# RWKV's outputs and its next state from one run of eight 96-column products

## The chip, the cores and the metric

One core of a Trainium2 chip runs the whole program in one launch. The metric is device time in microseconds (us); TensorE is called PE in the profile, its weight loads PEld, VectorE DVE, ScalarE ACT, GpSimd POOL, and SyncE's DMA issuing SP.

## The reference, cut to what matters

Two sequences, of 1024 and of 2048 tokens, each 1024 wide, go through an even layer and an odd one. The even layer has two branches side by side, an S5 state-space mixer and a bidirectional RWKV-7 mixer of 8 heads of 64, each gated. The odd layer is windowed attention. The change lies in the RWKV mixer, whose recurrence runs over every token, once in each direction:

```python
def step(S, inp):
    r_t, w_t, k_t, v_t, kk_t, b_t = inp
    sa = -jnp.einsum('bhvk,bhk->bhv', S, kk_t)
    S = (S * w_t[:, :, None, :] + sa[..., None] * b_t[:, :, None, :]
         + v_t[..., None] * k_t[:, :, None, :])
    return S, jnp.einsum('bhvk,bhk->bhv', S, r_t)

y = (rwkv_scan(R, tm(heads(decay(0))), K, V, KK, BB, False)
     + rwkv_scan(R, tm(heads(decay(1))), K, V, KK, BB, True))
```

## The kernel before, in words

All arithmetic is in f32. The program has four stages: input projections with the S5 branch, then `mixers`, then the even layer's output, then the odd layer with attention. Only `mixers` is changed. It holds two things: the RWKV recurrence (`rwkv`) and the gate products (`gates`: L887 for the gates, L970 for S5's last product, `h` and `w` being 128 columns wide).

The recurrence is cut into chunks of 32 tokens. The 3072 tokens make 96 chunks in each direction, so 192 in all; a block `h` of 128 tokens has four. For each chunk and each of the 8 heads `u` there is a weight matrix `lt[:, c1, u, :]` of 128 rows and 128 columns, and a right-hand side `rt[:, c1, u, :]` of 128 rows and 64 columns. One half of the rows holds the state, the other half the chunk's 32 values of `v` and 32 solved rows. Before the change the columns of `lt` are: 0 to 31 for the system's right-hand side, 32 to 63 for the outputs, 64 to 127 for the next state. `chain` walks the chunks of one direction in order, and for each one issues

- L1311, "U": eight products of 32 columns (four column groups of the array, each with its own quarter of the output partitions) into `pu`; ScalarE copies the result (L1314);
- L1320, "T": eight 32x32 products with the inverted system; ScalarE copies the solved rows into `rt` in four pieces (L1325);
- L1333 and L1334, "S": eight products of 64 columns, alternately in the two column halves; VectorE multiplies the result by the chunk's decay `wc` and writes it into the next chunk's `rt` (L1340, two instructions).

Beside the chain, `outputs` (L1356, "Y") forms the chunk's outputs: eight products of 32 columns from the same `lt` and `rt` into `pY`; ScalarE copies them into `ys` (L1363), and at a block's fourth chunk four transfers store `ys`. Other PE work of the recurrence is L1186/L1187 (`multiplied`, 64x64 quarters of the array), L1196 (transposes) and L1096 (decays).

In f32 each product appears in the trace as two matmul records and two weight loads, so eight products are 16 records.

The order on each engine is fixed when the program is built. `Plan.run` keeps a clock for each engine and, among the tasks whose inputs are ready, takes by rank and planned start; the gates have the lowest rank, 9. The costs in the `yield` lines are what the plan believes: `CC` 390 ns for U, T and Y, `CS` 620 ns for S, 225 ns for a gate product. `PACE` sets the planned distance between a chain's chunks, in hundredths of a us. `NEED` bears on how readily a gate product is put ahead of more urgent work: it is when the planned columns of PE's recent past come to less.

Of the kernel before, what the change touches and what calls it, by code (L numbers as in the profile page):

```python
# [19 lines left out]
P = 128  # L20
# [65 lines left out]
class Plan:  # L86
# [5 lines left out]
    SLACK = 0.25  # L92
    NEED = 3800
    ISSUE = 0.48
    AFTER = {"PE": 0.28, "SP": 0.0, "ACT": 0.1, "DVE": 0.14, "POOL": 0.1, None: 0.0}

    def __init__(self):
        self.clock = dict.fromkeys(self.AFTER, 0.0)
        self.queue = 0.0
        self.recent = deque()  # L100
        self.tasks = []
        self.now = 0.0
# [12 lines left out]
    def run(self):  # L115
        while self.tasks:
            best = {}
            for task in sorted(self.tasks, key=lambda x: x[0]):
                eng, cost, *waits = task[2]
                ts = [w if isinstance(w, float) else w.t for w in waits]  # L120
                if None in ts:
                    continue
                if eng == "SP":
                    n, cost = cost
                start = max(ts + [self.clock[eng] if eng else 0.0])
                if eng == "PE":
                    cost, cols = cost
                    if task[0] == 9 and eng in best and start <= best[eng][0] + 0.02:
                        end = start + best[eng][1]
                        if sum(c for t, c in self.recent if t > end - 3.413) + best[eng][2][2][1][1] < self.NEED:  # L130
                            best[eng] = start, cost, task
                            continue
                if eng not in best or (start < best[eng][0] and start + cost < best[eng][0] + self.SLACK):
                    best[eng] = start, cost, task
# [9 lines left out]
            else:  # L144
                if eng:
                    self.clock[eng] = start + cost
                if eng == "PE":
                    while self.recent and self.recent[0][0] < start - 4:
                        self.recent.popleft()
                    self.recent.append((start + cost, task[2][1][1]))  # L150
# [320 lines left out]
class Kern:  # L471
# [5 lines left out]
    GH = 2  # L477
    PACE, RF = 900, 9
    PACE2, LEFT = 600, 0
# [8 lines left out]
    RK, RT, RG2 = 1, 1, 2  # L488
    CG, CT, CC, CS, RG = 210, 230, 390, 620, 0
    B1, B2, B3, B4, KD = 2, 3, 1, 2, 0  # L490
# [494 lines left out]
    def rwkv_consts(self, cp):  # L985
# [6 lines left out]
        for d in range(2):  # L992
# [3 lines left out]
            for q in range(4):  # L996
                for c, base in ((0, -1), (32, 0)):
                    blk = tri[32 * q:32 * q + 32, c:c + 32]
                    nc.gpsimd.affine_select(out=blk, in_=blk, pattern=[[sg, 32]], compare_op=ALU.is_ge, fill=0.0, base=base, channel_multiplier=-sg)
# [15 lines left out]
        for i in range(self.NLT):  # L1015
            lt = cp.tile([P, 2, 8, P], F32, name=f"lt{i}")
            for c in range(2):
                nc.scalar.copy(lt[0:64, c, 4:8, 64:P], self.ident[0:64, 0:64].unsqueeze(1).broadcast_to([64, 4, 64]))
                nc.vector.tensor_copy(lt[64:P, c, 0:4, 64:P], self.ident[64:P, 64:P].unsqueeze(1).broadcast_to([64, 4, 64]))
            self.lts.append(lt)  # L1020
# [6 lines left out]
    def rwkv(self, plan, st):  # L1027
# [59 lines left out]
        def decays():  # L1087

            for h in every:
# [32 lines left out]
                h["decays"].mark(t)  # L1122
                tw = yield "DVE", 0.11, t1, ring_wc[d]
                h["wc free"] = ring_wc[d].take(4 if h["prev"] else 3)
                wc = ep.tile([P, 4, 4], F32, name=f"wc{d}", bufs=4)
                nc.vector.tensor_copy(wc, f1[:, :, :, 32 - e])
                h["wc"] = wc
                h["wc in"].mark(tw)

        def scaled():  # L1130

            for h in every:
# [20 lines left out]
                for c2 in range(2):  # L1153
                    cs = self.pair(d, c2)
                    slot, end = None, {}
                    for o in range(2):
                        rows = slice(64 * o, 64 * o + 64)
                        for n, at, off in ((2, 0, b), (0, 32, a)):
                            eng = "POOL" if n == 0 or o < self.APOOL else "DVE"
                            end[eng] = yield eng, 0.72 if eng == "POOL" else 0.455, t, *([] if slot else [ring_lt])  # L1160
                            if not slot:
                                slot, lt = ring_lt.take(2)
                                h["lt"][c2] = lt, slot
# [8 lines left out]
        def multiplied():  # L1172

            again = 0.0
            for i, h in enumerate(every):
                for c2 in range(2):
                    for c1 in range(2):
                        for p in range(4):
                            t = yield "PE", (self.CG / 1000, 128), h["keys"][c2], h["left"][c2], *([] if p else [again, *([] if c1 else [ring_g])])
                            if p == 0:  # L1180
                                again = plan.now + (self.GP / 100 if i > self.GI else 0)
                                if c1 == 0:
                                    gfree = ring_g.take()
                                    g = pg.tile([P, 2, 4, 64], F32, name="pg")
                                    (kb, kfree), (lt, _) = h["kb"][c2], h["lt"][c2]
                            nc.tensor.matmul(g[64:P, c1, p], kb[0:64, p, c1].rearrange("c s i -> c (s i)"), lt[0:64, c1, 4 + p, 0:64], start=True, stop=True)  # L1186
                            nc.tensor.matmul(g[0:64, c1, p], kb[64:P, p, c1].rearrange("c s i -> c (s i)"), lt[64:P, c1, p, 0:64], start=True, stop=True)  # L1187
                    plan.add(self.RK, masked(h, c2, g, lt, t, gfree))
# [14 lines left out]
        def masked(h, c2, g, lt, t, gfree):  # L1203
            t = yield "DVE", 1.3, t
            for rows, us in parts:
                nc.vector.tensor_tensor(lt[rows, :, us, 0:64], g[rows], self.tri[h["d"]][rows].unsqueeze(1).unsqueeze(1).broadcast_to([64, 2, 4, 64]), MULT)  # L1206
            gfree.mark(t)
# [3 lines left out]
        def turned(h, c2, g, lt, t, gfree):  # L1211
            for c1 in range(2):
                t = yield "ACT", 0.76, t
                for o, (rows, us) in enumerate(parts):
                    nc.scalar.copy(lt[rows, c1, us, 64:P], g[64 * c1:64 * c1 + 64, :, 64 * o:64 * o + 64])
                h["chunk"][2 * c2 + (c1 if h["d"] == 0 else 1 - c1)].mark(t)
            gfree.mark(t)

        def gathered(h, c2):
# [4 lines left out]
            for q in range(4):  # L1224
# [3 lines left out]
                put(win["ng"][32 * q:32 * q + 32, sys:sys + 4, :].rearrange("s (n j) t -> s n j t", j=2),  # L1228
                    lt[32 * q:32 * q + 32, :, 2 * q:2 * q + 2, 0:32])
            win["full"].mark(t)  # L1230
# [39 lines left out]
        def rights(hs):  # L1270

            for h in hs:
# [3 lines left out]
                for c2 in range(2):  # L1276
                    t = yield "POOL", 0.95, ring_rt[d]
                    rt = rp.tile([P, 2, 8, 64], F32, name=f"rt{d}")
                    h["rt"][c2] = rt, ring_rt[d].take(2)
                    nc.gpsimd.memset(rt, 0.0)  # L1280
# [12 lines left out]
        def chain(hs):  # L1293

            state = again = 0.0
            for h in hs:
# [3 lines left out]
                for ci in range(4):  # L1300
# [7 lines left out]
                    for j in range(2):  # L1308
                        for q in range(4):
                            u = 2 * q + j  # L1310
                            nc.tensor.matmul(pu[32 * q:32 * q + 32, j, :], lt[:, c1, u, 0:32], rt[:, c1, u, :], start=True, stop=True)  # L1311
                    t = yield "ACT", 0.26, t
# [10 lines left out]
                    for q in range(4):  # L1323
                        rows = slice(32 * q, 32 * q + 32)
                        nc.scalar.copy(rt[rows, c1, 2 * q:2 * q + 2, :], pu[rows, 2:4])  # L1325
                    plan.add(1, outputs(h, ci, c4, t, (ltfree, rtfree) if ci % 2 else ()))
                    nh = h if ci < 3 else h["next"]
                    if nh:
                        ni = (ci + 1) % 4
                        n4 = nat(ni)  # L1330
                        t = yield "PE", (self.CS / 1000, 1024), t
                        for p in range(4):
                            nc.tensor.matmul(pu[0:64, 4 + p, :], lt[:, c1, 4 + p, 64:P], rt[:, c1, 4 + p, :], start=True, stop=True)  # L1333
                            nc.tensor.matmul(pu[64:P, 4 + p, :], lt[:, c1, p, 64:P], rt[:, c1, p, :], start=True, stop=True)  # L1334
# [7 lines left out]
                    if ci % 2:  # L1342
                        ltfree.mark(t)
                        rtfree.mark(t)

        def outputs(h, ci, c4, t, frees):
            s, d, ti = h["s"], h["d"], h["ti"]
            c1, c2 = c4 % 2, ci // 2
            lt, rt = h["lt"][c2][0], h["rt"][c2][0]
# [7 lines left out]
            for x in frees:  # L1357
                x.mark(t)
            t = yield "ACT", 0.27, t, *([] if ci else [ring_ys[d]])
            if ci == 0:  # L1360
                h["y"] = ep.tile([P, 4, P], F32, name=f"ys{d}", bufs=1)
# [784 lines left out]
```

## Time and profile before

| what | value |
|---|---|
| median of 3 runs | 4057.42 us (4056.36 to 4058.29) |
| profiled execution: its time | 4065.39 us |
| its span | 4063.7 us |
| PE busy, share of the span | 3763.6 us, 93% |
| mean granted PE clock | 0.97 of full speed |

The profiled execution took 1.7 us more than its span, and 8 us more than the median of the runs. Busy PE time counts overlapping matmuls once.

### The profile page before, as it was taken

The numbers are of one execution on the slowest core, as the hardware profiler recorded it, in microseconds if no ns is written. First come the engines' busy times: TensorE is split into PE (matmuls) and PEld (weight loads), VectorE is DVE, ScalarE is ACT, GpSimd is POOL, SyncE is SP. The second block draws the span as 40 slices with busy tenths as digits, with TensorE's granted clock in tenths as the row PEclk, the third lists the DMA queues.
The fourth block names the chain that finished last, engine by engine and source line by source line (L and its number), as shares of the span: only waits on it lengthen the run. The fifth ranks groups of instructions, "written<-read, shape, count | busy, mean of one in ns | idle before, by whom it ended". The sixth has DMA issues, their size and how long they took to land.

```text
span 4063.7 us, 87721 instructions
## 1 busy us (share of the span) xinstructions
PE 3763.6 (93%) x34128; PEld 3118.4 (77%) x34128; DVE 2821.8 (69%) x5545; ACT 1939.8 (48%) x4847; POOL 1615.8 (40%) x2007
## 2 busy tenths in 40 slices
PE   6878999999899999999998799999999999999999
PEld 4656766676688888878876577999999977778777
DVE  8356655666568878888887676544444469899997
ACT  3334333333345565555655322333323357777776
POOL 4422322232364555555540242222222335555554
PEclk9989999999999999999999899999999999999999
DMA  5677565566543334333344666644444422222221
GB/s 154 162 174 228 162 191 173 174 191 188 176 154 101 119 112 127 119 106 115 119 115 98 216 233 214 206 148 155 143 157 147 147 84 72 77 81 74 76 66 58
DMA packets 536324, 570.32 MB, mean 140 GB/s; under 512 B 93602, under 2 KB 436770, under 8 KB 525924
## 3 DMA queue, kind: packets, MB, share of 16 engines
q1 hardware_dynamic: 535908, 564.72, 45.4%
q8 instruction: 268, 4.39, 0.5%
q14 instruction: 148, 1.21, 0.1%
HBM read 398.03 MB, written 166.56 MB: 139 GB/s over the span
## 4 chain that ended last, share of the span: by engine, by line
PE 45%; DVE 17%; DMA 4%; issue 4%; POOL 3%; ACT 2%; SPq 1%; DVEq 0%; ACTq 0%; POOLq 0%
PE ps L412 30%; DVE sb L412 11%; PE acc L887 5%; PE pc L1333 2%; PE acc L970 2%; PE pg L1186 2%; ACT sb L412 2%; DMA rk<-rk 1%; DVE ng L1251 1%; DVE z L1253 1%; PE pY L1356 1%; PE pc L1320 1%; POOL lt L1165 1%; PE pc L1311 1%; DVE lt L1206 1%
## 5 line engine op out<-in xcount | busy, mean ns | idle before, releaser
L412 PE MATMUL ps<-sb 128*128 128x512 f32 (+8 forms) x12464 | 2542.2, 359 | 153.2 <-DVE sb L412 48.4
L412 PEld LDWEIGHTS ps<-sb 128*128 128x128 f32 (+2 forms) x12464 | 1958.8, 187 | 555.7 <-DVE sb L412 105.0
L412 POOL TENSOR_TENSOR sb<-sb,sb 128x384 f32<-128x384 f32 (+5 forms) x468 | 469.5, 1021 | 444.2 <-ACT sb L412 226.0
L412 POOL TENSOR_TENSOR sb<-sb 128x512 f32<-128x512 f32 (+5 forms) x358 | 320.7, 899 | 675.0 <-ACT sb L412 325.8
L412 DVE TENSOR_TENSOR sb<-ps,sb 128x512 fp32r<-128x512 f32 (+4 forms) x620 | 402.0, 661 | 189.7 <-PE ps L412 115.5
L412 POOL TENSOR_TENSOR sb<-sb,mhalf 128x8 f32<-128x8 f32 (+3 forms) x156 | 223.0, 1431 | 644.4 <-DVE sb L412 640.5
L887 PE MATMUL acc<-h,w 128*128 128x128 f32 x3072 | 448.0, 290 | 17.0 <-POOL rt L1280 14.3
L887 PEld LDWEIGHTS acc<-h,w 128*128 128x128 f32 x3072 | 383.1, 196 | 42.5 <-POOL rt L1280 14.5
L412 ACT ACTIVATE sb<-sb 128x256 fp32r<-128x256 f32 (+9 forms) x392 | 276.1, 710 | 286.3 <-DVE sb L412 128.5
L412 ACT COPY sb<-ps 128x512 f32<-128x512 f32 (+4 forms) x402 | 195.1, 502 | 438.0 <-PE ps L412 429.3
L412 PE MATMUL ps<-ident,sb 128*128 128x128 f32 x1888 | 317.2, 280 | 55.5 <-DVE sb L412 51.1
L412 DVE TENSOR_TENSOR sb<-sb,sb 128x256 fp32r<-128x256 f32 (+6 forms) x259 | 265.8, 1038 | 142.9 <-ACT sb L412 128.8
L412 ACT ACTIVATE sb<-sb,sb 128x384 f32<-128x384 f32 (+3 forms) x486 | 299.3, 619 | 111.5 <-DVE sb L412 60.4
L412 PEld LDWEIGHTS ps<-ident,sb 128*128 128x128 f32 x1888 | 237.6, 143 | 119.9 <-DVE sb L412 72.1
L1165 POOL TENSOR_TENSOR lt<-rk,lb 64x256 f32<-64x256 f32 x288 | 216.9, 761 | 196.3 <-PE pY L1356 84.8
L412 ACT ACTIVATE sb<-ps 128x512 f32<-128x512 f32 x108 | 64.5, 597 | 385.7 <-PE ps L412 385.7
L1325 ACT COPY rt<-pc 32x128 f32<-32x128 f32 x768 | 196.7, 256 | 97.7 <-PE pc L1320 86.6
L412 DVE CUSTOM_DVE_ANT_0 sb<-ps,sb,sb 128x384 f32<-128x384 f32 (+1 forms) x384 | 215.3, 588 | 28.6 <-PE ps L412 27.1
L1150 POOL TENSOR_TENSOR kb<-rk,f 128x128 f32<-128x128 f32 x384 | 197.6, 546 | 76.1 <-PE pg L1196 67.6
L412 ACT CAST sb<-ps 128x512 fp32r<-128x512 f32 x368 | 202.1, 587 | 50.9 <-PE ps L412 46.0
L1340 DVE TENSOR_TENSOR rt<-pc,wc 64x256 f32<-64x256 f32 x376 | 158.3, 421 | 71.5 <-PE pc L1334 36.1
L412 DVE TENSOR_SCALAR sb<-sb,sb 128x384 f32<-128x384 f32 (+4 forms) x264 | 190.6, 751 | 18.2 <-POOL sb L412 16.2
(121 smaller groups left out, 4680.1 us busy)
## 6 DMA issues: line engine op xcount, KB each, us to landing
sb<-wsp SPq DMA_DIRECT2D x65, 1024.0 KB
rk<-rk SPq DMA_DIRECT2D x96, 512.0 KB
sb<-in_od_w_in SPq DMA_DIRECT2D x36, 1024.0 KB
h<-h SPq DMA_DIRECT2D x48, 512.0 KB
sb<-in_od_w_z SPq DMA_DIRECT2D x24, 1024.0 KB
qkv<-sb SPq DMA_DIRECT2D x72, 256.0 KB
sb<-qkv SPq DMA_DIRECT2D x72, 256.0 KB
sb<-in_x_sample SPq DMA_DIRECT2D x32, 512.0 KB
```

The costliest lines, as they stand in the source:

```text
L412: self.ops.append((eng, self.cost(eng, op, outs[-1] if outs[-1] is not k.get("accum_out") else outs[0], ins, a, k), deps, self.rank, lambd ...
L887: nc.tensor.matmul(sums[n][1][:, m * P:m * P + P], w[:, k, m * P:m * P + P], acts[n][0][:, k], start=k == 0, stop=k == KT - 1)
L970: nc.tensor.matmul(ps[:, 256 * (m % 2):256 * (m % 2) + 256], uw_at(k)[:, m], act_at(n)[:, 2 * k:2 * k + 2], start=k == 0, stop=k == 3)
L1150: nc.gpsimd.tensor_tensor(kb[:, sl, :, x, :], arr[n][:, sl, cs], f1[:, sl, cs, a:a + 32], MULT)
L1165: (nc.gpsimd if eng == "POOL" else nc.vector).tensor_tensor(ltv[:, :, :, at:at + 32], arr[n][rows, :, cs], f2[rows, :, cs, off:off + 32], ...
L1186: nc.tensor.matmul(g[64:P, c1, p], kb[0:64, p, c1].rearrange("c s i -> c (s i)"), lt[0:64, c1, 4 + p, 0:64], start=True, stop=True)
L1206: nc.vector.tensor_tensor(lt[rows, :, us, 0:64], g[rows], self.tri[h["d"]][rows].unsqueeze(1).unsqueeze(1).broadcast_to([64, 2, 4, 64]), MULT)
L1251: nc.vector.tensor_tensor(tv, z[:, 0:k, k:k + 1].broadcast_to([P, k, 31 - k]), z[:, k:k + 1, k + 1:32].broadcast_to([P, k, 31 - k]), MULT)
L1253: nc.vector.tensor_tensor(z[:, 0:k, k + 1:32], z[:, 0:k, k + 1:32], tv, ADD)
L1325: nc.scalar.copy(rt[rows, c1, 2 * q:2 * q + 2, :], pu[rows, 2:4])
L1333: nc.tensor.matmul(pu[0:64, 4 + p, :], lt[:, c1, 4 + p, 64:P], rt[:, c1, 4 + p, :], start=True, stop=True)
L1340: nc.vector.tensor_tensor(nrt[rows, n4 % 2, 4 - 4 * o:8 - 4 * o, :], pu[rows, 4:8], nh["wc"][rows, :, n4:n4 + 1].broadcast_to([64, 4, 64]) ...
```

## The change

The columns of `lt` are turned round: the next state's 64 columns now stand first, then 32 for the outputs, then 32 for the right-hand side of the system. S and Y become one run, Z: for each of the 8 heads one product of 96 columns into 96 partitions of a full PSUM bank `pz`, rows 0 to 63 the next state, rows 64 to 95 the outputs. VectorE reads the state for both head groups from partitions 0 to 63, so the decay `wc` is kept on 64 partitions and is filled by two copies. ScalarE copies the outputs as 32 partitions of 512 columns into the block's row of `ys`, which one transfer then stores. In the plan, Z costs `CS` 900 ns and 2048 columns, a PE task costs `TURN` 95 ns more when it is 128-wide work (gates or Z) behind other work or the other way round, `NEED` is 3000, `PACE` 800, and the store is planned 0.5 us behind the copy and no longer 2.0.

```diff
-    NEED = 3800
+    NEED = 3000
+    TURN = 0.095
...
+                    cost += self.TURN * (self.wide != (task[0] == 9 or cols == 2048))
...
+                    self.wide = task[0] == 9 or task[2][1][1] == 2048
...
-    PACE, RF = 900, 9
+    PACE, RF = 800, 9
...
-    CG, CT, CC, CS, RG = 210, 230, 390, 620, 0
+    CG, CT, CC, CS, RG = 210, 230, 390, 900, 0
+    YL = 0.5
...
-                tw = yield "DVE", 0.11, t1, ring_wc[d]
+                tw = yield "DVE", 0.22, t1, ring_wc[d]
...
-                wc = ep.tile([P, 4, 4], F32, name=f"wc{d}", bufs=4)
-                nc.vector.tensor_copy(wc, f1[:, :, :, 32 - e])
+                wc = ep.tile([64, 2, 4, 4], F32, name=f"wc{d}", bufs=4)
+                for o in range(2):
+                    nc.vector.tensor_copy(wc[:, o], f1[64 * o:64 * o + 64, :, :, 32 - e])
...
-                    plan.add(1, outputs(h, ci, c4, t, (ltfree, rtfree) if ci % 2 else ()))
+                    t = yield "PE", (self.CS / 1000, 2048), t, ring_y
+                    yfree = ring_y.take(2)
+
+                    pz = py.tile([P, 8, 64], F32, name="pz")
+                    for u in range(8):
+                        nc.tensor.matmul(pz[0:96, u, :], lt[:, c1, u, 0:96], rt[:, c1, u, :], start=True, stop=True)
+                    if ci % 2:
+                        ltfree.mark(t)
+                        rtfree.mark(t)
+                    plan.add(1, outputs(h, ci, c4, pz, t, yfree))
...
-                        t = yield "PE", (self.CS / 1000, 1024), t
-                        for p in range(4):
-                            nc.tensor.matmul(pu[0:64, 4 + p, :], lt[:, c1, 4 + p, 64:P], rt[:, c1, 4 + p, :], start=True, stop=True)
-                            nc.tensor.matmul(pu[64:P, 4 + p, :], lt[:, c1, p, 64:P], rt[:, c1, p, :], start=True, stop=True)
-                        tm = t
                         state = t = yield "DVE", 0.87, t, nh["wc in"], nh["right"][ni // 2]
                         nrt = nh["rt"][ni // 2][0]
                         for o in range(2):
-                            rows = slice(64 * o, 64 * o + 64)
-                            nc.vector.tensor_tensor(nrt[rows, n4 % 2, 4 - 4 * o:8 - 4 * o, :], pu[rows, 4:8], nh["wc"][rows, :, n4:n4 + 1].broadcast_to([64, 4, 64]), MULT)
+                            us = slice(4 - 4 * o, 8 - 4 * o)
+                            nc.vector.tensor_tensor(nrt[64 * o:64 * o + 64, n4 % 2, us, :], pz[0:64, us], nh["wc"][:, o, :, n4:n4 + 1].broadcast_to([64, 4, 64]), MULT)
                         nh["wc free"].mark(t)
...
-            t = yield "PE", (self.CC / 1000, 512), t, ring_y
-            yfree = ring_y.take()
-            pY = py.tile([P, 2, 64], F32, name="pY")
-            for j in range(2):
-                for q in range(4):
-                    u = 2 * q + j
-                    nc.tensor.matmul(pY[32 * q:32 * q + 32, j, :], lt[:, c1, u, 32:64], rt[:, c1, u, :], start=True, stop=True)
...
-            t = yield "ACT", 0.27, t, *([] if ci else [ring_ys[d]])
+            t = yield "ACT", 0.53, t, *([] if ci else [ring_ys[d]])
...
-            nc.scalar.copy(h["y"][:, c4, :], pY.rearrange("r j v -> r (j v)"))
+            nc.scalar.copy(h["y"][32 * c4:32 * c4 + 32], pz[64:96].rearrange("i u v -> i (u v)"))
...
-                t = yield "SP", (4, 0.73), t + 2.0
-                dst = self.sp[s]["y"][d][ti].rearrange("(n i) c -> i n c", i=32)
-                for q in range(4):
-                    nc.sync.dma_start(dst[:, :, q * P:(q + 1) * P], h["y"][32 * q:32 * q + 32])
+                t = yield "SP", (1, 0.73), t + self.YL
+                nc.sync.dma_start(self.sp[s]["y"][d][ti], h["y"])
```

Left out of this diff are the lines that only follow the new order of the columns (the masks `tri`, the identity blocks in `lt`, the slices in `scaled`, `multiplied`, `masked`, `turned`, `gathered` and U) and the counts of readers of `lt` and `rt`, which fall from two to one.

## Rows read from the trace of the kernel before

**Rows 1.** The profile's page: span, busy time of each engine.
```profile
span 4063.7 us, 87721 instructions
...
PE 3763.6 (93%) x34128; PEld 3118.4 (77%) x34128; DVE 2821.8 (69%) x5545; ACT 1939.8 (48%) x4847; POOL 1615.8 (40%) x2007
```

**Rows 2.** Windows: us; busy PE, PEld, DVE, ACT, POOL; PEclk; DMA share; GB/s.
```profile
1245.00:2268.00 1023.00, 961.71 (x18161) 798.52 (x18162) 833.34 (x1736) 600.04 (x1913) 484.02 (x744) 0.97 0.39 112
...
1250.00:2050.00 800.00, 762.76 (x14873) 648.93 (x14873) 672.15 (x1406) 474.10 (x1538) 439.62 (x685) 0.98 0.38 116
```

**Rows 3.** TensorE's timeline (start, duration, work): one place, first and last state runs.
```profile
1251.70 0.27 PE L1333 MATMUL pc<-rt,lt 128*64 128x64 f32 x1
...
1611.87 0.27 PE L1333 MATMUL pc<-rt,lt 128*64 128x64 f32 x1
...
1611.97 0.22 PE L1333 MATMUL pc<-rt,lt 128*64 128x64 f32 x1
...
1612.32 0.22 PE L1333 MATMUL pc<-rt,lt 128*64 128x64 f32 x1
...
1612.48 0.43 PE L1356 MATMUL pY<-rt,lt 128*32 128x64 f32 x16
1612.84 0.94 PE L887 MATMUL acc<-h,w 128*128 128x128 f32 x6
1613.71 0.43 PE L1311 MATMUL pc<-rt,lt 128*32 128x64 f32 x16
...
2049.30 0.27 PE L1333 MATMUL pc<-rt,lt 128*64 128x64 f32 x1
```

**Rows 4.** The same timeline elsewhere: two kinds alike in line, a longer gate run.
```profile
1608.53 0.43 PE L1311 MATMUL pc<-rt,lt 128*32 128x64 f32 x16
1608.78 0.41 PE L1356 MATMUL pY<-rt,lt 128*32 128x64 f32 x16
1609.11 0.71 PE L887 MATMUL acc<-h,w 128*128 128x128 f32 x4
...
1619.88 2.05 PE L887 MATMUL acc<-h,w 128*128 128x128 f32 x16
1621.86 0.27 PE L1333 MATMUL pc<-rt,lt 128*64 128x64 f32 x1
```

**Rows 5.** TensorE's timeline: 128-column weights under two streamed columns, two places.
```profile
562.62 0.72 PE L412 MATMUL ps<-heads,sb 128*128 128x2 f32 x6
563.21 2.74 PE L412 MATMUL ps<-sb 128*128 128x512 f32 x14
...
1077.00 1.17 PE L412 MATMUL ps<-heads,sb 128*128 128x2 f32 x10
1078.04 2.29 PE L412 MATMUL ps<-sb 128*128 128x512 f32 x9
```

**Rows 6.** Lines L1333 and L887: weight loads, ns least, median, most.
```profile
L1333 PEld LDWEIGHTS pc<-rt,lt x1504: 132/138/232, 1245.7 to 2261.0; 128*64 128x64 f32 x188
...
L887 PEld LDWEIGHTS acc<-h,w x3072: 186/192/338, 1114.1 to 2073.7; 128*128 128x128 f32 x192
```

**Rows 7.** Groups by line and form: busy us, mean ns, idle before.
```profile
L1325 ACT COPY rt<-pc 32x128 f32<-32x128 f32 x768 | 196.7, 256 | 97.7 <-PE pc L1320 86.6 <-DMA twt<-tw 1.1 <-DMA rt<-v 1.0
...
L1340 DVE TENSOR_TENSOR rt<-pc,wc 64x256 f32<-64x256 f32 x376 | 158.3, 421 | 71.5 <-PE pc L1334 36.1 <-issue 15.1 <-ACT rt L1325 9.8
...
L412 ACT COPY sb<-ps 64x512 f32<-64x512 f32 x96 | 55.8, 581 | 31.0 <-PE ps L412 29.1
...
L1363 ACT COPY ys<-pY 128x128 f32<-128x128 f32 x192 | 50.6, 265 | 88.9 <-PE pY L1356 71.1 <-issue 5.9 <-DMA y<-ys 5.7
...
L1126 DVE COPY wc<-f 128x16 f32<-128x16 f32 x48 | 12.8, 266 | 0.8 <-ACT f L1117 0.4
```

**Rows 8.** Waits by engine and line: us in total, times, longest.
```profile
POOL rt L1280 <- PE pY L1356: 104.7, 18, 18.1
```

**Rows 9.** Transfers issued between 1400 and 2000 us.
```profile
y<-ys SPq DMA_DIRECT2D x111, 64.0 KB
```

More of the change, by code (lines that the diff above doesn't have):

```diff
@@ L100, in __init__ @@
         self.recent = deque()
+        self.wide = False
         self.tasks = []
@@ L996, in rwkv_consts @@
             for q in range(4):
-                for c, base in ((0, -1), (32, 0)):
+                for c, base in ((32, -1), (0, 0)):
                     blk = tri[32 * q:32 * q + 32, c:c + 32]
@@ L1017, in rwkv_consts @@
             for c in range(2):
-                nc.scalar.copy(lt[0:64, c, 4:8, 64:P], self.ident[0:64, 0:64].unsqueeze(1).broadcast_to([64, 4, 64]))
-                nc.vector.tensor_copy(lt[64:P, c, 0:4, 64:P], self.ident[64:P, 64:P].unsqueeze(1).broadcast_to([64, 4, 64]))
+                nc.scalar.copy(lt[0:64, c, 4:8, 0:64], self.ident[0:64, 0:64].unsqueeze(1).broadcast_to([64, 4, 64]))
+                nc.vector.tensor_copy(lt[64:P, c, 0:4, 0:64], self.ident[64:P, 64:P].unsqueeze(1).broadcast_to([64, 4, 64]))
             self.lts.append(lt)
@@ L1157, in scaled @@
                         rows = slice(64 * o, 64 * o + 64)
-                        for n, at, off in ((2, 0, b), (0, 32, a)):
+                        for n, at, off in ((2, 96, b), (0, 64, a)):
                             eng = "POOL" if n == 0 or o < self.APOOL else "DVE"
@@ L1161, in scaled @@
                             if not slot:
-                                slot, lt = ring_lt.take(2)
+                                slot, lt = ring_lt.take()
                                 h["lt"][c2] = lt, slot
@@ L1185, in multiplied @@
                                     (kb, kfree), (lt, _) = h["kb"][c2], h["lt"][c2]
-                            nc.tensor.matmul(g[64:P, c1, p], kb[0:64, p, c1].rearrange("c s i -> c (s i)"), lt[0:64, c1, 4 + p, 0:64], start=True, stop=True)
-                            nc.tensor.matmul(g[0:64, c1, p], kb[64:P, p, c1].rearrange("c s i -> c (s i)"), lt[64:P, c1, p, 0:64], start=True, stop=True)
+                            nc.tensor.matmul(g[64:P, c1, p], kb[0:64, p, c1].rearrange("c s i -> c (s i)"), lt[0:64, c1, 4 + p, 64:P], start=True, stop=True)
+                            nc.tensor.matmul(g[0:64, c1, p], kb[64:P, p, c1].rearrange("c s i -> c (s i)"), lt[64:P, c1, p, 64:P], start=True, stop=True)
                     plan.add(self.RK, masked(h, c2, g, lt, t, gfree))
@@ L1205, in masked @@
             for rows, us in parts:
-                nc.vector.tensor_tensor(lt[rows, :, us, 0:64], g[rows], self.tri[h["d"]][rows].unsqueeze(1).unsqueeze(1).broadcast_to([64, 2, 4, 64]), MULT)
+                nc.vector.tensor_tensor(lt[rows, :, us, 64:P], g[rows], self.tri[h["d"]][rows].unsqueeze(1).unsqueeze(1).broadcast_to([64, 2, 4, 64]), MULT)
             gfree.mark(t)
@@ L1214, in turned @@
                 for o, (rows, us) in enumerate(parts):
-                    nc.scalar.copy(lt[rows, c1, us, 64:P], g[64 * c1:64 * c1 + 64, :, 64 * o:64 * o + 64])
+                    nc.scalar.copy(lt[rows, c1, us, 0:64], g[64 * c1:64 * c1 + 64, :, 64 * o:64 * o + 64])
                 h["chunk"][2 * c2 + (c1 if h["d"] == 0 else 1 - c1)].mark(t)
@@ L1228, in gathered @@
                 put(win["ng"][32 * q:32 * q + 32, sys:sys + 4, :].rearrange("s (n j) t -> s n j t", j=2),
-                    lt[32 * q:32 * q + 32, :, 2 * q:2 * q + 2, 0:32])
+                    lt[32 * q:32 * q + 32, :, 2 * q:2 * q + 2, 96:P])
             win["full"].mark(t)
@@ L1278, in rights @@
                     rt = rp.tile([P, 2, 8, 64], F32, name=f"rt{d}")
-                    h["rt"][c2] = rt, ring_rt[d].take(2)
+                    h["rt"][c2] = rt, ring_rt[d].take()
                     nc.gpsimd.memset(rt, 0.0)
@@ L1310, in chain @@
                             u = 2 * q + j
-                            nc.tensor.matmul(pu[32 * q:32 * q + 32, j, :], lt[:, c1, u, 0:32], rt[:, c1, u, :], start=True, stop=True)
+                            nc.tensor.matmul(pu[32 * q:32 * q + 32, j, :], lt[:, c1, u, 96:P], rt[:, c1, u, :], start=True, stop=True)
                     t = yield "ACT", 0.26, t
@@ L1338, in chain, with outputs @@
                         for o in range(2):
-                            rows = slice(64 * o, 64 * o + 64)
-                            nc.vector.tensor_tensor(nrt[rows, n4 % 2, 4 - 4 * o:8 - 4 * o, :], pu[rows, 4:8], nh["wc"][rows, :, n4:n4 + 1].broadcast_to([64, 4, 64]), MULT)
+                            us = slice(4 - 4 * o, 8 - 4 * o)
+                            nc.vector.tensor_tensor(nrt[64 * o:64 * o + 64, n4 % 2, us, :], pz[0:64, us], nh["wc"][:, o, :, n4:n4 + 1].broadcast_to([64, 4, 64]), MULT)
                         nh["wc free"].mark(t)
[L1342 to L1346, printed above, removed]
+                    yfree.mark(t)
+        def outputs(h, ci, c4, pz, t, yfree):
             s, d, ti = h["s"], h["d"], h["ti"]
-            c1, c2 = c4 % 2, ci // 2
-            lt, rt = h["lt"][c2][0], h["rt"][c2][0]
-            t = yield "PE", (self.CC / 1000, 512), t, ring_y
-            yfree = ring_y.take()
-            pY = py.tile([P, 2, 64], F32, name="pY")
-            for j in range(2):
-                for q in range(4):
-                    u = 2 * q + j
-                    nc.tensor.matmul(pY[32 * q:32 * q + 32, j, :], lt[:, c1, u, 32:64], rt[:, c1, u, :], start=True, stop=True)
-            for x in frees:
-                x.mark(t)
-            t = yield "ACT", 0.27, t, *([] if ci else [ring_ys[d]])
+            t = yield "ACT", 0.53, t, *([] if ci else [ring_ys[d]])
             if ci == 0:
-                h["y"] = ep.tile([P, 4, P], F32, name=f"ys{d}", bufs=1)
+                h["y"] = ep.tile([P, 512], F32, name=f"ys{d}", bufs=1)
                 h["y free"] = ring_ys[d].take()
-            nc.scalar.copy(h["y"][:, c4, :], pY.rearrange("r j v -> r (j v)"))
+            nc.scalar.copy(h["y"][32 * c4:32 * c4 + 32], pz[64:96].rearrange("i u v -> i (u v)"))
             yfree.mark(t)
             if ci == 3:
-                t = yield "SP", (4, 0.73), t + 2.0
-                dst = self.sp[s]["y"][d][ti].rearrange("(n i) c -> i n c", i=32)
-                for q in range(4):
-                    nc.sync.dma_start(dst[:, :, q * P:(q + 1) * P], h["y"][32 * q:32 * q + 32])
+                t = yield "SP", (1, 0.73), t + self.YL
+                nc.sync.dma_start(self.sp[s]["y"][d][ti], h["y"])
                 h["y free"].mark(t)
```

## The prediction

> **What bounds the kernel now.** I read the page first, then windows over the stage that changes, then PE's timeline inside it. The page says that PE is busy for 93% of the span and no other engine for more than 69% [rows 1]. The windows say the same of the changed stage: the recurrence runs from 1245 to 2268 us, 1023 us for 96 chunks in each direction, so 10.66 us for one step of both chains, and PE is busy for 961.7 us of it. 61 us are left over. VectorE is busy for 833, ScalarE for 600, POOL for 484 [rows 2]. The granted clock is 0.97 there. So in this stage time follows what PE has to do, and the change must be priced in PE time between the start of one run of products and the start of the next. Busy time won't do for that, as neighbouring records overlap.
>
> The timeline gives those starts. S begins at 1611.87, its second pair comes 0.10 later, and from 1611.97 to the last pair at 1612.32 six steps take 0.35, so 0.058 us for a pair; Y begins at 1612.48, so S takes 0.61. Y to the gate run behind it takes 0.36 [rows 3]. Where U is followed by Y, of the same shape, U takes only 0.25 [rows 4]: 0.11 of the 0.36 is the change to another kind of product. A gate run of six records takes 0.87 up to U [rows 3], one of sixteen 1.98 up to S [rows 4]: 0.111 for a record, and 0.87 - 6 x 0.111 = 0.20 that does not grow with the run, 0.10 for each of its two changes of kind.
>
> **What a chunk costs on PE now.** S 0.61 and Y 0.36, of which 0.11 is saved where U follows. Counted in the timeline from 1250 to 2050 us, of 148 S runs [rows 3] 103 have 128-wide work ahead of them, and of 148 Y runs 74 have it behind them and 19 have U. With 0.10 for each change out of or into 128-wide work: 0.61 + 0.10 x 103/148 + 0.36 - 0.11 x 19/148 + 0.10 x 74/148 = 0.61 + 0.07 + 0.35 + 0.05 = 1.08 us. That is what goes.
>
> **What Z costs.** The run has 16 records, each of 96 weight columns under 64 streamed columns. No such record is in the trace, so it is bounded from both sides. If the stream sets the pace, a record costs what 64 columns cost in S, 0.058, and Z 16 x 0.058 = 0.93. If the weight load sets the pace, the row to ask is one with many weight columns and hardly any stream. There is one: the norm's products with `heads`, 128 weight columns under two streamed ones. Six records take 0.59 us and ten 1.04 [rows 5], so four more take 0.45, 0.112 for a record: as much as a gate record, which streams 128 columns. Two columns cannot take that long to stream; the load of 128 weight columns does, and the next record waits for it. The duration of one load grows from 138 ns for 64 columns to 192 ns for 128 [rows 6], 0.84 ns for a column, so 96 columns should take 32 x 0.84 = 27 ns less than 128: 0.112 - 0.027 = 0.085 for a record and 16 x 0.085 = 1.36 us for Z. Until now the narrow products hid this, since S and Y load two and four column groups beside each other: S has 64 columns in each half and still needs only 0.058 for two records [rows 3].
>
> A rule speaks against the change: the Trainium skill, "TensorE: Matmul & The Clock Gate", section "LDWEIGHTS (loading the stationary operand)", gives a load's time as the number of its columns divided by 1.2 per ns, whatever the number of rows. As an estimate from that page Z would be 16 x 80 ns = 1.28 us in place of my 1.36, and the loss below smaller by 15 us; the rows above are longer by some 5 ns a record than the rule, and the sum goes by them.
>
> I take 1.36, since the `heads` row is the one case here in which the load has no stream to hide behind; 0.93 stays as the lower bound. Upper bound: if 96 columns load no faster than 128, 16 x 0.112 = 1.79. I give that little, as load times do follow the columns [rows 6].
>
> Z is 128-wide like the gates, so changes of kind go where Z stands beside them. With the neighbours of S and Y as counted, 45/148 of the Z runs have narrow work ahead and half have it behind: 0.10 x 0.30 + 0.10 x 0.50 = 0.08. Z with its changes: 1.44. PE gains 1.44 - 1.08 = 0.36 us for a chunk, and 192 chunks make +70 us.
>
> **What of that is time.** Of the 61 us in which PE stands idle in this stage [rows 2], a part goes if PE itself is later than its suppliers: the plan believes in 0.9 us plus 0.095 for a change, so POOL, VectorE and the loads are laid out for a PE that is faster than the real one. Not all goes, as the last chunks wait on their own chain. I take half, 30 us: +70 - 30 = +40. None and all of it are the bounds: +70 and +9.
>
> **The other parts.** ScalarE's copy of the outputs goes from 128x128 at 265 ns to 32 rows of 512; the nearest row is a 64x512 copy at 581 ns [rows 7]. That is 192 x 0.32 = 61 us more on an engine that is idle for 423 of the 1023 us [rows 2]. It costs nothing while it lies beside PE. Queued behind it are the copies of U and T of the other chain: if each such copy held up a chain, a step of 10.66 us would still have room. That step needs U 0.36, its copy 0.27, T 0.36, four copies of 0.256, Z 1.44 and two VectorE products of 0.42 [rows 3, 7], 4.3 us and the handovers. VectorE has 48 more small copies of `wc`, 0.27 each [rows 7], 13 us off the path. SP issues 3 x 48 = 144 transfers fewer; the stores were 64 KB each [rows 9] and are one of 256 KB for a block now. The store is issued 1.5 us earlier in the plan; if the copy is late, SP waits, and behind it stand the loads of `rk`, `v` and the gates' activations. I put the two together at nothing, and at 10 us either way for the range. `lt` and `rt` come free behind Z and not behind the later Y; POOL's clearing of `rt` waited 104.7 us for Y [rows 8], but POOL is busy for under half of the stage, so what it gains is slack. `PACE` 800 asks for 8 us between chunks where PE delivered 10.66: it moves recurrence ahead of gates and takes no work off PE. The two VectorE products read PSUM in the same sizes as before, 0.
>
> **The sum.** The profiled execution took 4065.4 us; with +40 it is 4105. The runs' median lies 8 us below it, so the forecast is 4057.4 + 40 = 4097 us.
>
> **The rivals.** *The stream sets the pace after all (other side).* Then Z is 0.93 + 0.08 = 1.01 against 1.08, -0.07 for a chunk, and between 128-wide neighbours 0.93 against 0.10 + 0.61 + 0.36 + 0.10 = 1.17, -0.24: -13 to -46 us, so 4011 to 4044, middle 4028. For it speaks that changes of kind cost a real 0.10, measured in the gate runs, and that each Z saves one or two of them. Against it stands the `heads` row. It decides from the record's price: with 1.08 - 0.08 = 1.00 us left for 16 records, Z breaks even at 0.0625 us a record before any idle time is absorbed, and at about 0.072 with it (30 us over 192 chunks are 0.16 us).
>
> *The load sets the pace, but it doesn't show.* All 61 us of idle time go, or the plan, retimed, puts gates on both sides of Z: then 1.36 against 1.17, +0.19 x 192 = +36, less what is absorbed. 4052 to 4065.
>
> *Worse: the clock.* `NEED` 3000 puts fewer gate products ahead of the chain, and PE's mix of work changes with Z. If the stage's granted clock fell from 0.97 [rows 2] to 0.93, that is 4% of 1023 us, 41 us on top: 4138.
>
> **How the numbers follow.** A change within 0.2% (8 us) cannot be told from none here. Load-bound Z with half of the idle time taken, 0.54: 4066 to 4127 by the bounds, slower. Stream-bound Z, 0.31: faster. Load hidden by slack, 0.10: the same in 0.08, slower in 0.01, faster in 0.01. Clock, 0.05: slower. Faster 0.32, same 0.08, slower 0.60. The range from 4025 to 4128 takes in the likeliest case and more than half of the rival below it, and leaves out the lower end of that rival and the clock. The likeliest case's own range is 4066 to 4127.
>
> **What would show each step.** Z's records: 0.085 us apart, or 0.058. Z from start to next start beside the gates 1.36. No gap between Z and a gate run. PE busy in the stage above 94% and the stage from 1245 us on longer by some 40 us, with the other stages as they are. ScalarE's copy at about 0.58. The chain's step above 10.66 us with its waits still on PE. I am wrong if Z takes under 1.0 us, or if the stage's time doesn't follow PE's work.

## The result and the profile after

The changed kernel takes 4144.47 us (median of 4 runs, 4141.55 to 4150.86) against 4056.89 for the kernel before, run beside it: a ratio of 1.0216, 95% interval 1.0201 to 1.0231. That is 87.6 us slower, where 40 were forecast, and beyond the range. The profiled execution took 4143.15 us, 77.8 more than that of before.

The page, a window over the stretch of [rows 2], and the groups by line and form:

```profile
span 4141.2 us, 81618 instructions
...
PE 3815.2 (92%) x31120; PEld 3223.2 (78%) x31120; DVE 2850.2 (69%) x5593; ACT 2002.3 (48%) x4847; POOL 1589.1 (38%) x2007
```
```profile
1245.00:2268.00 1023.00, 950.00 (x14656) 850.32 (x14655) 815.72 (x1702) 622.21 (x1824) 460.91 (x743) 0.97 0.34 104
```
```profile
L1361 ACT COPY ys<-pz 32x512 f32<-32x512 f32 x192 | 110.7, 578 | 186.4 <-DVE rt L1351 87.1 <-PE pz L1338 83.4 <-PE pc L1318 5.9
...
L1133 DVE COPY wc<-f 64x16 f32<-64x16 f32 x96 | 27.4, 285 | 1.9 <-ACT f L1123 1.1
```

Two things stand against each other. PE has more work: 51.6 us more busy time in the whole program [rows 1]. Yet in the changed stage it is *less* busy than before, 950 us of the 1023 against 961.7 [rows 2]. The granted clock is 0.97 as before. So PE got more to do and was kept from doing it; the forecast had only the first.

TensorE's timeline shows one Z run from its start to the next start, and the lines of Z's load, of S5's last product (L976; L970 before) and of U show where the stage ends:

```profile
1606.92 1.49 PE L1338 MATMUL pz<-rt,lt 128*96 128x64 f32 x16
1608.34 0.27 PE L1193 MATMUL pg<-lt,kb 64*64 64x64 f32 x1
```
```profile
L1338 PEld LDWEIGHTS pz<-rt,lt x3072: 159/165/283, 1235.8 to 2282.1; 128*96 128x96 f32 x192
...
L976 PE MATMUL acc<-w x384: 379/379/796, 2203.0 to 2347.6; 128*128 128x256 f32 x192
...
L1318 PE MATMUL pc<-rt,lt x3072: 216/219/316, 1137.4 to 2278.3; 128*32 128x64 f32 x192
```

Z takes 1.42 here (ahead of narrow work it is either 1.42 or 1.50), and 1.33 as the median of some 60 runs that stand between 128-wide work: 0.083 us for a record. Its load lies between those of [rows 6]. The recurrence's last U starts at 2278.3. In the kernel before, the same two lines read:

```profile
L970 PE MATMUL acc<-w x384: 379/379/796, 2077.4 to 2256.3; 128*128 128x256 f32 x192
...
L1311 PE MATMUL pc<-rt,lt x3072: 216/219/316, 1143.4 to 2265.1; 128*32 128x64 f32 x192
```

There the last U starts at 2265.1, and S5's product was done before the recurrence ended, its last record at 2256.3; now that record starts at 2347.6. So the two chains end only 13 us later, but the low-ranked products that fill their gaps no longer fit in them, and the last of them run behind the chains for some 70 us.

The waits hold something that [rows 7] doesn't have. ScalarE's copy of the outputs waits for VectorE, and VectorE for ScalarE's copy:

```profile
ACT ys L1361 <- DVE rt L1351: 87.1, 61, 4.6
...
DVE rt L1351 <- ACT ys L1361: 51.3, 57, 4.2
...
PEld pc L1327 <- ACT u L1321: 36.9, 45, 3.9
...
PE pc L1327 <- ACT u L1321: 27.2, 35, 3.7
```

Both engines read the same PSUM bank `pz`, VectorE rows 0 to 63 and ScalarE rows 64 to 95, and the program lets one go only when the other is through. In the kernel before they read two tiles, `pu` and `pY`. PE comes into it in the last two rows: T waits for ScalarE's copy of U, 27.2 us in all. In the kernel before that wait was small:

```profile
PE pc L1320 <- ACT u L1314: 3.6, 7, 0.9
```

A stretch of the timeline of all engines shows how:

```profile
1549.57 1.49 PE L1338 MATMUL pz<-rt,lt 128*96 128x64 f32 x16
...
1550.49 0.71 DVE L1260 TENSOR_TENSOR z<-z,ng 128x220 f32<-128x220 f32 x1
1550.99 0.43 PE L1318 MATMUL pc<-rt,lt 128*32 128x64 f32 x16
1551.13 0.41 DVE L878 SCALAR_TENSOR_TENSOR z<-z,acc 128x256 f32<-128x256 f32 x1
1551.46 0.62 DVE L1258 TENSOR_TENSOR ng<-z 128x228 f32<-128x228 f32 x1
...
1551.57 0.38 ACT L876 ACTIVATE z<-acc 128x256 f32<-128x256 f32 x1 [1.76 <-DVE z L878]
...
1552.33 0.84 DVE L1351 TENSOR_TENSOR rt<-pz,wc 64x256 f32<-64x256 f32 x2
...
1553.26 0.58 ACT L1361 COPY ys<-pz 32x512 f32<-32x512 f32 x1 [1.31 <-DVE rt L1351]
...
1553.86 0.27 ACT L1321 COPY u<-pc 128x128 f32<-128x128 f32 x1
...
1554.18 0.53 PE L1327 MATMUL pc<-u,tt 32*32 32x64 f32 x16 [2.15 <-ACT u L1321]
```

Z ends at about 1551.0. VectorE still has other work in its queue and reads the state only from 1552.33 to 1553.17. ScalarE ends a gate's activation at 1551.95 and could copy the outputs then, but stands for 1.31 us until VectorE is through; behind that copy in its queue stands the copy of U, whose product has been done since 1551.4, and behind that T on PE, which idles for 2.15 us.

### The profile page after: what moved, and what is told of

The parts are those of the page before. It is cut to its first block, busy times and chain, and to the rows that moved or that the text cites. A ratio compares the mean times of both kernels' runs of the same rounds, so it can differ in the third digit from the quotient of the medians.

```text
span 4141.2 us, 81618 instructions
## 1 busy us (share of the span) xinstructions
PE 3815.2 (92%) x31120; PEld 3223.2 (78%) x31120; DVE 2850.2 (69%) x5593; ACT 2002.3 (48%) x4847; POOL 1589.1 (38%) x2007
## 5 line engine op out<-in xcount | busy, mean ns | idle before, releaser
L893 PE MATMUL acc<-h,w 128*128 128x128 f32 x3072 | 429.7, 287 | 16.3 <-DMA w<-in_ev_w_zr 14.0
L1338 PE MATMUL pz<-rt,lt 128*96 128x64 f32 x3072 | 299.7, 252 | 0.2 <-ACT rt L1332 0.2
L1338 PEld LDWEIGHTS pz<-rt,lt 128*96 128x96 f32 x3072 | 287.4, 169 | 6.8 <-ACT rt L1332 0.4
L1351 DVE TENSOR_TENSOR rt<-pz,wc 64x256 f32<-64x256 f32 x376 | 156.2, 415 | 134.0 <-PE pz L1338 75.8
L417 DVE CUSTOM_DVE_ANT_0 sb<-ps,sb,sb 128x384 f32<-128x384 f32 (+1 forms) x384 | 215.5, 588 | 27.2 <-PE ps L417 25.5
L1157 POOL TENSOR_TENSOR kb<-rk,f 128x128 f32<-128x128 f32 x384 | 178.8, 496 | 133.3 <-PE pg L1203 106.5
```

The lines of the kernel that those rows point to most:

```text
L417: self.ops.append((eng, self.cost(eng, op, outs[-1] if outs[-1] is not k.get("accum_out") else outs[0], ins, a, k), deps, self.rank, lambd ...
L893: nc.tensor.matmul(sums[n][1][:, m * P:m * P + P], w[:, k, m * P:m * P + P], acts[n][0][:, k], start=k == 0, stop=k == KT - 1)
L1157: nc.gpsimd.tensor_tensor(kb[:, sl, :, x, :], arr[n][:, sl, cs], f1[:, sl, cs, a:a + 32], MULT)
L1338: nc.tensor.matmul(pz[0:96, u, :], lt[:, c1, u, 0:96], rt[:, c1, u, :], start=True, stop=True)
L1351: nc.vector.tensor_tensor(nrt[64 * o:64 * o + 64, n4 % 2, us, :], pz[0:64, us], nh["wc"][:, o, :, n4:n4 + 1].broadcast_to([64, 4, 64]), MULT)
```

## The experiments

The theories: *(L)* the weight load makes Z long, and PE's time is the program's; *(P)* the plan's numbers (`CS`, `NEED`, `PACE`, `TURN`) made a worse order; *(B)* the bank that two engines read costs waits that the plan does not hold. The runs were made on other chips, where the kernel before took 4070 to 4075 us, so only ratios to the kernel before on the same chip are compared; 0.01 is 41 us.

**Z without the long load (z32).** Three products of 32 columns in three column groups, in place of one of 96, all else as after:
```diff
-                        nc.tensor.matmul(pz[0:96, u, :], lt[:, c1, u, 0:96], rt[:, c1, u, :], start=True, stop=True)
+                        for e in range(0, 96, 32):
+                            nc.tensor.matmul(pz[e:e + 32, u, :], lt[:, c1, u, e:e + 32], rt[:, c1, u, :], start=True, stop=True)
```


> Only Z's products change: each 96-column product becomes three of 32 columns, in three column groups beside each other; plan, order, buffers and all other work stay. If the weight loads set Z's price (0.083 us a record, 1.33 us a run), three short loads run side by side and the run costs what its stream costs, 16 x 0.058 = 0.93 plus about 0.13 for leaving the kind, and more changes against the gates: some 0.25 to 0.3 us less a chunk, 45 to 60 us in all, about 4090 us. If instead the stream or the bank of eight heads set it, Z stays near 1.4 us and the time near 4144.

Ratio 1.0175 (1.016 to 1.019). The timeline confirms the load, the time does not follow it:

```profile
1609.00 1.09 PE L1339 MATMUL pz<-rt,lt 128*32 128x64 f32 x48
1610.02 0.43 PE L1327 MATMUL pc<-u,tt 32*32 32x64 f32 x16
```
```profile
PEld pc L1327 <- ACT u L1321: 53.4, 57, 5.0
...
PE pc L1327 <- ACT u L1321: 40.5, 41, 4.9
```

The same 96 columns and the same stream take 1.02 us, so it was the load. All Z runs together fall from 280 to 197 us, 83 less, but only 0.0041, 17 us, come back. Counted as in the table further down, the gate runs, which now stand beside another kind of product, take 20 us of it, so that PE's work in the stage falls by 58; and PE's idle time grows by 35, of which 15 stand ahead of T and 12 ahead of U. (L) is right on the price and wrong on what the time follows.

**The plan's numbers.** With Z's planned cost at its measured one (cs1330), and with the old `PACE` and `NEED` (oldplan); and alone on the kernel before, where only the gates count as wide (newplan):
```diff
-    CG, CT, CC, CS, RG = 210, 230, 390, 900, 0
+    CG, CT, CC, CS, RG = 210, 230, 390, 1330, 0
```


> The changed kernel with the plan's price of Z at 1330 ns, what it takes on the chip, in place of 900. If the growth of PE's idle time (70 to 96 us in the stage) comes from an order laid out for a Z that is too cheap, idle falls back by 15 to 25 us: about 4120. If it comes from the waits between ScalarE and VectorE for Z's bank, or from the new distances between chunks, it stays near 4144.


```diff
-    NEED = 3000
+    NEED = 3800
...
-    PACE, RF = 800, 9
+    PACE, RF = 900, 9
```


> The changed kernel with PACE 900 and NEED 3800 as before. If the earlier chain, which leaves S5's last products alone at the end of the stage (2282 to 2347 us), costs time, the stage gets 10 to 15 us shorter, about 4130. If Z's own price is all, the time stays within 8 us of 4144.


```diff
-    NEED = 3800
+    NEED = 3000
+    TURN = 0.095
...
+                    cost += self.TURN * (self.wide != (task[0] == 9))
...
-    PACE, RF = 900, 9
+    PACE, RF = 800, 9
```


> The kernel before with the new numbers of the plan alone (TURN, NEED 3000, PACE 800). If the numbers by themselves make an order that costs time, 1.003 to 1.01; if, as the run with the old numbers suggests (27 us slower than the changed kernel), they help or are neutral, 0.996 to 1.001.

Ratios 1.0407 (1.0387 to 1.0427), 1.0282 (1.0254 to 1.0309), and 1.005 (1.0031 to 1.0068). The honest `CS` is much the worst. Its S5 product, and windows ahead of it and over it:

```profile
L976 PE MATMUL acc<-w x384: 379/379/796, 2316.1 to 2436.3; 128*128 128x256 f32 x192
```
```profile
2275.00:2316.00 41.00, 29.23 (x246) 28.88 (x244) 6.62 (x12) 5.03 (x11) 0.00 (x0) 0.88 0.43 115
2316.00:2436.00 120.00, 94.64 (x382) 78.30 (x383) 49.95 (x80) 42.04 (x68) 0.00 (x0) 0.91 0.48 99
```

The last Z starts at 2270.7. Behind it come gates until 2306 and then 120 us of S5's product: a plan that believes PE full leaves less room for rank 9, which then runs alone behind the chains. The granted clock is lower too, 0.94 in the stage of [rows 2] where after has 0.97, and no run tells how much of the loss that is. The old `PACE` and `NEED` make the changed kernel slower by 27 us, where a gain was expected; the new numbers alone make the old kernel slower by 20. The numbers are not neutral, and what they are worth depends on the kernel they are in. `TURN` was not tried by itself.

**The wait for the bank, planned (statefirst).** The outputs' task is entered behind the state's products, so that the plan has the order that the bank can give:
```diff
-                    plan.add(1, outputs(h, ci, c4, pz, t, yfree))
...
                         yfree.mark(t)
+                    plan.add(1, outputs(h, ci, c4, pz, t, yfree))
```


> The changed kernel with the copy of the outputs planned behind the product that makes the next state, so that VectorE never waits for ScalarE's 0.58 us read of the same bank; PE's work is the same. If that wait on the chain's way (51 us in 57 places) feeds PE's idle time, 10 to 20 us go: about 4130. If PE's work alone sets the time, or ScalarE's wait for VectorE (87 us) is the one that hurts, no gain or a loss of up to 10 us.

Ratio 1.0112 (1.0092 to 1.0133): 42 us back from a move of one line. Its waits:

```profile
ACT ys L1361 <- DVE rt L1350: 130.1, 92, 5.8
...
PEld pc L1327 <- ACT u L1321: 4.5, 12, 0.7
...
PE pc L1327 <- ACT u L1321: 1.1, 3, 0.4
```

The outputs' copy waits for VectorE *longer* than after, 130.1 us against 87.1, and yet the kernel is the faster one: in ScalarE's queue the copy of U now stands right ahead of it in 69 of 192 places, in after in 42, and T's wait has nearly gone. With z32's products as well (sf_z32):

> Both edits at once: Z as 24 products of 32 columns, and the outputs copied behind the state. Alone the first took 83 us of PE work out of Z and gave back only some 17 us, with PE then idle for 60 us more, waiting for ScalarE's copy of U; the second gave back some 42 us. If PE's work and the waits for Z's bank are the two causes and the waits were what hid the first, the two together give back nearly all: ratio to the kernel before 0.995 to 1.003. If something else holds the chain (the distances between chunks, the single ring of banks), PE stays idle and the ratio stays at 1.005 or more.

Ratio 1.0034 (1.0023 to 1.0046). The three 32-column products are worth 0.0078, 32 us, in this order, against 17 in that of after; the planned order is worth 57 us to z32 and 42 to after.

**The opposite order, and no common bank.** If state-first won because the state is on the chain, outputs-first (outfirst) must lose. And with the outputs' columns in a bank of their own (z32_2banks, one buffer of each in place of two common ones) z32's wait must go whatever the order:
```diff
+                    copied = Event()
-                    plan.add(1, outputs(h, ci, c4, pz, t, yfree))
+                    plan.add(1, outputs(h, ci, c4, pz, t, yfree, copied))
...
-                        state = t = yield "DVE", 0.87, t, nh["wc in"], nh["right"][ni // 2]
+                        state = t = yield "DVE", 0.87, t, copied, nh["wc in"], nh["right"][ni // 2]
...
+            copied.mark(t)
```


> The changed kernel with the opposite order: in every chunk the state's product is planned behind the copy of the outputs, 0.58 us, as the shared bank forced in 57 places of the changed kernel. If this wait on the chain is what cost some 35 us there, making it the rule costs more: ratio 1.025 to 1.04. If PE's work alone sets the time, 1.0216 as for the changed kernel.


```diff
+                    po = py.tile([P, 8, 64], F32, name="po")
...
+                            nc.tensor.matmul((pz if e < 64 else po)[e:e + 32, u, :], lt[:, c1, u, e:e + 32], rt[:, c1, u, :], start=True, stop=True)
...
-                    plan.add(1, outputs(h, ci, c4, pz, t, yfree))
+                    plan.add(1, outputs(h, ci, c4, po, t, ofree))
```


> z32 with the bank split: the state's two column groups go to one PSUM bank, the outputs' to another, so ScalarE and VectorE need not wait for each other in either order. To stay in eight banks, each of the two is single and the two chains share it. z32 gave 1.0175; with the copy behind the state it gave 1.0034. If the shared bank is the wait that the reordering took away, 1.002 to 1.008 here without that reordering; if only the order mattered, 1.015 or more, and more still if the single banks hold up the other chain.

Outfirst gives 1.0115 (1.0098 to 1.0132), the same as statefirst, although VectorE's state waits 80.0 us for the copy there. My expectation of a loss fell, and with it the idea that the 0.58 us on the chain were the cost. Two banks give 1.0057 (1.0039 to 1.0075), 48 us better than z32. The waits of outfirst, then of two banks:

```profile
DVE rt L1352 <- ACT ys L1362: 80.0, 71, 4.9
PEld pc L1327 <- ACT u L1321: 6.3, 16, 1.8
...
PE pc L1327 <- ACT u L1321: 1.9, 2, 1.6
```
```profile
ACT ys L1364 <- PE po L1341: 114.9, 91, 5.0
...
PE pz L1341 <- DVE rt L1354: 54.2, 36, 6.1
```

With two banks the copy waits for PE alone, and PE pays 54.2 us for the single buffers. What statefirst, sf_z32, outfirst and the two banks share is that the plan knows in which order the readers of a bank come, or that they need none. (B) stands, in this form.

**The old `PACE` and `NEED` on the planned order (sf_oldplan).** The diffs of oldplan and statefirst together:

> The copy behind the state, with PACE 900 and NEED 3800 as before. The new numbers cost the kernel before 0.5%, while the old ones cost the changed kernel 0.7%. If the new numbers are a loss wherever the bank's wait is gone, 1.005 to 1.009 against 1.0112; if they suit the heavier PE work, 1.012 to 1.02.

Ratio 1.0143 (1.0126 to 1.016), 13 us slower than statefirst, though the two intervals overlap a little. With Z in the kernel its own numbers are the better ones, clearly so in after.

**The stores (st4).** Four stores of 32 rows in place of one, planned 2.0 us behind the copy:
```diff
-    YL = 0.5
+    YL = 2.0
...
-                t = yield "SP", (1, 0.73), t + self.YL
-                nc.sync.dma_start(self.sp[s]["y"][d][ti], h["y"])
+                t = yield "SP", (4, 0.73), t + self.YL
+                for q in range(4):
+                    nc.sync.dma_start(self.sp[s]["y"][d][ti][32 * q:32 * q + 32], h["y"][32 * q:32 * q + 32])
```


> The changed kernel with each block's outputs stored by four transfers of 32 rows, planned 2.0 us behind the copy, as the kernel before did. If the stores and SP's queue don't lie on the way, within 10 us of the changed kernel (ratio 1.019 to 1.024); if the single early store holds up the loads behind it, up to 20 us faster; if four issues hold up SP, slower.

Ratio 1.0206 (1.0187 to 1.0226): no effect that can be told from after's.

**The other way round on the kernel before (s32, s32cs).** If narrow loads beside each other are what counts, S gains from two 32-column products in place of one of 64; s32cs also lowers its planned cost from 620 to 510 ns:
```diff
-                            nc.tensor.matmul(pu[0:64, 4 + p, :], lt[:, c1, 4 + p, 64:P], rt[:, c1, 4 + p, :], start=True, stop=True)
-                            nc.tensor.matmul(pu[64:P, 4 + p, :], lt[:, c1, p, 64:P], rt[:, c1, p, :], start=True, stop=True)
+                            for e in range(4):
+                                u = 4 + p if e < 2 else p
+                                nc.tensor.matmul(pu[32 * e:32 * e + 32, 4 + p, :], lt[:, c1, u, 64 + 32 * (e % 2):96 + 32 * (e % 2)], rt[:, c1, u, :], start=True, stop=True)
```


> The kernel before with S alone rewritten: each 64-column product as two of 32 columns, four column groups beside each other, so that U, S and Y are one kind. Streams and loads side by side as before (0.464 us), but S to Y needs no change of kind: some 0.11 to 0.14 us less for most of 188 runs, 16 to 25 us of PE work, and since PE's work sets this kernel's time, a ratio of 0.994 to 0.997. If the changes of kind are not what these gaps are, 1.0.

> s32 (0.9984) with the plan told what S takes there, 510 ns and not 620; the work is the same. In s32 PE lost 23 us of work and gained 9 us of idle time. If an order that knows the price turns that into time, 0.994 to 0.997; if the order is as good as any, 0.998; an order can also come out worse by luck, as other numbers did by up to 1%.

S falls from 0.61 to 0.47 us ahead of Y:

```profile
1616.01 0.65 PE L1335 MATMUL pc<-rt,lt 128*32 128x64 f32 x32
1616.48 0.41 PE L1357 MATMUL pY<-rt,lt 128*32 128x64 f32 x16
```

The ratio is 0.9984 (0.9973 to 0.9995), 6 us faster than the kernel before, the best that was found and within what I called no change; 16 to 25 us had been expected. S saves 21 us over the stage (117.5 to 96.6 us). With the smaller planned cost nothing is left, 1.0002 (0.9988 to 1.0017).

## Why the prediction was wrong

The direction and the price of Z were right; the size was less than half. I counted the timelines of four kernels from the first gate product (1114.1 us in the kernel before, 1108.6 in after) to the end of the stage's last product (2268.3 and 2348.0): what no product covers is idle, the rest is PE's work.

| kernel | PE's work, us | idle, us | both, against before | by the ratio, us |
|---|---|---|---|---|
| before | 1082 | 72 | – | – |
| newplan: the plan's numbers | 1064 | 110 | +20 | +20 |
| statefirst: and Z, the bank's order planned | 1129 | 69 | +44 | +45 |
| after: and the bank's order unplanned | 1141 | 98 | +85 | +88 |

*PE's cost.* 0.085 us for a record was forecast, 0.083 measured; 1.36 us beside gates, 1.33 measured. From newplan to statefirst the work grows by 65 us, close to the forecast's +70. The rule of the Trainium skill in "TensorE: Matmul & The Clock Gate", "LDWEIGHTS (loading the stationary operand)", gives, as an estimate from that page, 80 ns for 96 columns. Here the pace of the records lies between it and my estimate, and agrees that the columns of the weights set the time; the row of a single load is longer, 165 ns in the median.

*"What of that is time", the step that failed.* I let half of PE's idle time absorb 30 us. From newplan to statefirst the idle time does fall, by 41, so that Z by itself costs 24 us there and not 40. But the step took the idle time as otherwise fixed, and two things that I had priced at nothing moved it. The plan's numbers ("it moves recurrence ahead of gates and takes no work off PE") took 18 us off PE's work, with 305 runs of gate and S5 products in place of 457 and so fewer changes of kind, and added 38 of idle. And "the two VectorE products read PSUM in the same sizes as before, 0" looked at sizes and not at who else reads the bank: from statefirst to after idle grows by 29 and work by 12, 41 us, 42 by the ratio. In all the idle term was +26 (72 to 98) in place of -30, and PE's work +59 in place of +70: 85 in place of 40. The shared bank was the larger cause. Statefirst, which lacks only its unplanned wait, took 45 us, which a forecast of 40 nearly hits, but that would have been luck: its work grew by 47 where 70 was forecast, and its idle time fell by 3 where 30 was.

*Could it be luck of the order?* Every edit that plans the bank's order also makes a new order, and new numbers alone moved the time by 13 to 78 us, so luck can't be ruled out for any one run. T's wait on PE for the copy of U speaks against it: it is 23 to 41 us in the five kernels with the bank's order unplanned (after, z32, cs1330, oldplan, st4), and 0.4 to 4.5 us in the five with it planned or with two banks (statefirst, sf_z32, outfirst, sf_oldplan, z32_2banks). And from after to statefirst PE's idle time just ahead of T falls from 34 to 5 us, and that is all by which its idle time in the stage falls (98 to 69).

*ScalarE.* The copy was forecast at 0.58 us and takes 0.578. I had seen that the copies of U queue behind it and left a chunk's step room for that. The chain had the room, but PE had not: each such wait is a hole in PE's fixed order, and gates that could fill it stand behind the waiting T.

*The Trainium skill,* "PSUM — Partial Sum Buffer", "PSUM bank collisions raise a hardware error", says that two engines must not touch one bank in one group of 32 partitions at a time, reads included, and that different groups could go side by side. State and outputs lie in different groups here, 0 to 63 and 64 to 95; this program orders all readers of the bank, and no run let them read together, so that part is open.

*The rest.* The rival "stream sets the pace" fell with Z's 1.33. "Hidden by slack" fell, since the slack grew. "Clock" fell: 0.97 in both. The stores at nothing were right, as st4 shows; `wc`'s copies take 27.4 us on VectorE, 14.6 more than before where 13 were foreseen, and no run shows what that is worth. "PE busy in the stage above 94%" was the sign that told: it is 92.9%. The range of "hidden by slack", 4052 to 4065, does not follow from its own terms: 61 us off the +70 make 4066, and 61 off the +36 make 4032. Nothing else hangs on it.

What stays open is the share of `TURN`, `NEED` and `PACE` apart from each other. The rows of the table are one profiled execution each, and the plan's term depends on the kernel: newplan loses 20 us, while the old `PACE` and `NEED` lose 13 in statefirst and 27 in after.

## What to carry to other kernels

When two results are put into one PSUM bank, ask which engines read it and whether the schedule knows that they read one after the other: in engines that work in order, a wait that the plan doesn't hold can hold up whatever is queued behind it, and here a longer wait that the plan held was in the faster kernel. Joining narrow products into one wide one gives up loads that ran beside each other in column groups, so price the run by its weight columns, not by its instructions. In a planned order, work added to the bound engine doesn't simply eat idle time; price the retimed plan as a term of its own, and watch where the low-ranked filler ends.

## What was not expected of the hardware

Three 32-column loads in three column groups, each under 64 streamed columns, take 1.02 us for eight heads where one of 96 takes 1.42 or 1.50 ahead of narrow work and 1.33 beside gates. For 64 columns in S the step to 32-column products still saves 0.14 us a run ahead of Y (0.61 to 0.47). Of the 83 us of PE time that z32 took out of Z, only 17 came back with the unplanned waits in place, and 32 without them; in both orders, each planned with Z at 900 ns as before, PE's idle time grew by some 35.
